# Row maxima of grouped heads: one product of 128 rows per head, or two of 64 rows side by side

## The chip, the cores and the metric

The kernel runs on one core of one Trainium2 chip. The metric is the device time of one execution, in microseconds (us); lower is better. A core has five engines with queues of their own: TensorE (PE; its weight loads are listed as PEld), VectorE (DVE), ScalarE (ACT), GpSimd (POOL) and SyncE (SP), which here starts the DMAs. TensorE writes its products to PSUM, eight banks of 128 partitions x 512 numbers.

## The reference

Two layers of an encoder trunk on 512 tokens of width 1024, in float32. Each layer has three branches on the normed input (latent attention, grouped-query attention, pooling), each projected, gated and added, an output projection, and a gated feed-forward part with a depthwise convolution. The change concerns the grouped-query branch: 8 query heads of 64, 2 key heads, so four query heads share a key head.

```python
def gqa_branch(q_raw, k_raw, v_raw, qn_g, kn_g, cos, sin):
    q = q_raw.reshape(b, s, GQA_HEADS, GQA_HEAD_DIM)
    k = k_raw.reshape(b, s, GQA_KV_HEADS, GQA_HEAD_DIM)
    q = apply_rope(rms_norm(q, qn_g), cos, sin)
    k = apply_rope(rms_norm(k, kn_g), cos, sin)
    o = block_attention(q, k, v)
...
def one_block(qi):
    sc = jnp.einsum('bqgrd,bkgd->bgrqk', qi, k) * scale
    p = jax.nn.softmax(sc, axis=-1)
    return jnp.einsum('bgrqk,bkgv->bqgrv', p, v)
```

The softmax needs a number to subtract from each row of scores before the exponential. It cancels in the quotient, so it has only to be near the row's maximum.

## The kernel before, in words

**Precision.** Numbers are split into a high half (rounded to the format that TensorE multiplies in one pass) and a low half (the rest). A full product is three: high by high, high by low, low by high (`mm3`, L347). Weights stream from HBM through SP's queue into `raw`; ScalarE makes their high halves `wh`, GpSimd or VectorE the low halves `wl`.

**The order is written by a planner.** The program has no loop on the chip: Python writes every instruction, and each engine runs its own in that order. While it writes, a model (`Clock`) keeps estimated times of the engines and of events. `chain` places the steps that follow a product (evacuations, copies, subtractions) into the queues when the model's time comes; `need(key)` moves the model's time to the moment when an event is estimated to be over; `ps(tag)` does the same for a free PSUM bank. PSUM has five tags: acc (2 banks), ST (2), AV (2), S (1) and mi (1). None of these estimates is seen by the chip: it only sees the order and its own semaphores.

**Attention.** `attention(kind, fill, ...)` runs once for grouped heads ("gqa") and once for latent heads ("mla") in each layer. Its steps are sorted by a position. One unit of position is one block of 128 keys, and head h has its scores at 4h to 4h+3:

- `t_q` (for grouped heads `t_pair`): four transposes bring the queries of two heads into mi. Then, head by head: `hi` copies 64 partitions out of mi into `qa`; `lo` subtracts, mi less the copy, into the other 64 partitions of `qa`, and copies the high half to `qb`. After the second head's subtraction mi is free. The order is hi, hi, lo, lo.
- `s_max`(h, b): scores of 128 queries by all 512 keys into bank S, and a `tensor_reduce` on VectorE that writes the negated row maximum into column b of `nm`.
- `m_row`(h): a product with the identity turns `nm` into rows (bank mi), which VectorE writes into four rows of `qb`.
- `probs`(h, k): scores with keys on the partitions, in ST, with the maxima subtracted by those rows; exponential, high half `ph`, low half `pl`.
- `av_hi`, `av_lo`: products with the values into AV; `o_out` after the last: copies, four reciprocals, a product, a split.

For grouped heads `qa` has high and low half of a head's queries on its 128 rows, and `ka` has the keys' high half twice, on rows 0 to 63 and 64 to 127. The even head of a pair has its high half on rows 0 to 63, the odd one on rows 64 to 127.

Between the steps stands **filler**: products of gates and branches that don't depend on this attention, in steps of mostly three products of 512 columns. Ahead of each attention step filler is made up to a target that grows with the position (positions below 0 count by PRO = 0.47). For grouped heads it has 104 steps in all, of which 16 (PRE_A) are made before. Then, as long as the step would have to wait by the planner's estimate, further filler steps are made, up to 35 (SLACK) ahead of the target. What a step waits for is told by `waits`: a list of events and one bank.

```python
PLAN = {"gqa": (0.006, 0.786, 0.986, 0.65, 3.252, 2.411, 4.57, 32.003),
...
            tq, tk, s0, ds, mr, ah, al, end = PLAN[kind]
```

With p0 = 4(h - 1), `t_q` stands at p0 + 0.006, the maxima at p0 + 0.986 + 0.65k, `m_row` at p0 + 3.252, `av_hi` at 4h + k + 2.411 and `av_lo` at 4h + k + 4.57.

## Time and profile before

| | |
|---|---|
| three runs | 1660.67, 1662.70, 1664.17 us |
| their median | 1662.7 us |
| profiled execution: its own time | 1662.54 us |
| profiled execution: span of the trace | 1660.7 us |
| products on TensorE | 7394 |
| reductions for maxima on VectorE | 128 of 684 ns (mean) |
| products for maxima of grouped heads | 64, in `ps_S<-ka,qa` |
| bytes moved by DMA | 145.40 MB |

How to read it: a row of the timeline gives start, duration, engine, line, operation, what it writes and reads, tile, shape, and how many neighbouring instructions were merged; behind it, in brackets, stands how long the engine sat idle before and what ended that. Line numbers are often those of helpers: L340 is `mm`, L344 the transposes, L208 ScalarE, L215 a `tensor_tensor`, L223 a reduction. Products are told apart by their tiles. Of a product the record's end is modelled, so records overlap; the distance of starts is what one costs. In the windows the last three columns are the granted clock of TensorE as a share, the DMA share and GB/s.

### The profile page before, as it was taken

The page shows a single profiled execution, that of the slowest core. Times are in us where ns is not written, and L with a number is a line of the kernel's source. Part 1 is how long each engine was busy: PE and PEld are TensorE (multiplying, and loading weights), DVE is VectorE, ACT ScalarE, POOL GpSimd, SP SyncE. Part 2 cuts the span into 40 slices and gives each one's busy share as a digit, 9 for nine tenths or more (in the row PEclk, how much of TensorE's full clock was granted, in tenths as well). Part 3 has the DMA queues.
Part 4 walks back from the last instruction along what each step waited for, and adds up shares of the span by engine and source line. Part 5 has one row for each costly group of instructions (what it writes and reads, how often), then busy time and mean ns, then how long its engine had stood idle before and what let it go on. Part 6 is the DMA issues. An engine that isn't in the chain of part 4 may idle for free.

```text
span 1660.7 us, 20300 instructions
## 1 busy us (share of the span) xinstructions
PE 1648.2 (99%) x7394; PEld 1339.3 (81%) x7394; DVE 918.7 (55%) x1428; ACT 773.2 (47%) x1366; POOL 921.5 (55%) x787
## 2 busy tenths in 40 slices
PE   9999999999999999999999999999999999999999
PEld 9887787778888888888888877877788888888887
DVE  6677866753356667621046678667542666666100
ACT  6357755553444444433244567555434444444221
POOL 4752754444666566654567537533546666666543
PEclk9999999999999999999999999999999999999999
DMA  5231121124333333233333211211232222323331
GB/s 179 89 96 36 58 74 51 38 64 134 108 89 93 98 92 99 89 114 108 103 103 99 73 37 56 73 52 38 83 126 99 99 90 90 101 90 99 110 115 57
DMA packets 44596, 145.40 MB, mean 88 GB/s; under 512 B 5073, under 2 KB 6353, under 8 KB 44497
## 3 DMA queue, kind: packets, MB, share of 16 engines
q1 hardware_dynamic: 44352, 144.10, 27.4%
q8 instruction: 58, 0.95, 0.2%
q14 instruction: 42, 0.34, 0.1%
q10 hardware_dynamic: 144, 0.01, 0.0%
HBM read 139.90 MB, written 4.19 MB: 87 GB/s over the span
## 4 chain that ended last, share of the span: by engine, by line
PE 96%; DVE 2%; ACT 1%; POOL 1%; issue 0%; POOLq 0%; DVEq 0%
PE ps_acc L340 42%; PE ps_ST L340 24%; PE ps_AV L340 24%; PE ps_S L340 3%; PE ps_mi L340 2%; PE ps_mi L344 1%; PE ps_mi L1395 0%; POOL wl L215 0%; POOL MQ L215 0%; DVE nm L223 0%; DVE rp L215 0%; DVE kb L215 0%; ACT ps_ST L208 0%; DVE pl L215 0%; ACT ph L208 0%
## 5 line engine op out<-in xcount | busy, mean ns | idle before, releaser
L215 POOL TENSOR_TENSOR wl<-raw,wh 128x512 fp32r<-128x512 f32 (+3 forms) x508 | 665.5, 1319 | 601.4 <-ACT wh L208 511.4
L208 ACT ACTIVATE wh<-raw 128x512 fp32r<-128x512 f32 (+3 forms) x522 | 314.9, 609 | 190.1 <-PE ps_ST L340 82.9
L219 DVE SCALAR_TENSOR_TENSOR a<-u,prm,a 128x512 f32<-128x512 f32 x176 | 240.8, 1369 | 79.4 <-ACT a L208 72.8
L340 PE MATMUL ps_acc<-HH,wh 128*128 128x512 f32 x592 | 234.5, 396 | 0.8 <-DVE XM L219 0.8
L340 PE MATMUL ps_acc<-HL,wh 128*128 128x512 f32 x592 | 234.5, 396 | 0.0
L340 PE MATMUL ps_acc<-HH,wl 128*128 128x512 f32 x592 | 233.9, 395 | 0.5 <-POOL wl L215 0.5
L340 PEld LDWEIGHTS ps_acc<-HH,wh 128*128 128x128 f32 x592 | 111.4, 188 | 28.1 <-issue 1.2
L340 PEld LDWEIGHTS ps_acc<-HH,wl 128*128 128x128 f32 x592 | 111.3, 188 | 27.5 <-POOL wl L215 1.0
L208 ACT ACTIVATE ps_ST<-ps_ST 128x512 f32<-128x512 f32 x128 | 74.6, 583 | 126.2 <-PE ps_ST L340 125.3
L340 PEld LDWEIGHTS ps_acc<-HL,wh 128*128 128x128 f32 x592 | 111.4, 188 | 25.6
L340 PE MATMUL ps_AV<-HL,wh 128*128 128x512 f32 x288 | 114.2, 396 | 0.0
L340 PE MATMUL ps_AV<-HH,wl 128*128 128x512 f32 x288 | 114.1, 396 | 0.0
L340 PE MATMUL ps_AV<-HH,wh 128*128 128x512 f32 x288 | 113.5, 394 | 0.0
L223 DVE TENSOR_REDUCE nm<-ps_S 128x1 fp32r<-128x512 f32 x128 | 87.5, 684 | 33.1 <-PE ps_S L340 32.1
L215 POOL TENSOR_TENSOR al<-a,ah 128x512 fp32r<-128x512 f32 x44 | 58.1, 1322 | 84.7 <-ACT ah L208 60.5
L215 DVE TENSOR_TENSOR pl<-ps_ST,ph 128x512 fp32r<-128x512 f32 x128 | 86.7, 679 | 30.4 <-ACT ph L208 29.4
L340 PE MATMUL ps_ST<-HL,wh 128*128 128x512 f32 x240 | 95.2, 396 | 0.0
L340 PE MATMUL ps_ST<-HH,wl 128*128 128x512 f32 x240 | 94.9, 396 | 0.0
L340 PE MATMUL ps_ST<-HH,wh 128*128 128x512 f32 x240 | 94.6, 394 | 0.0
L208 ACT ACTIVATE a<-u,prm 128x512 f32<-128x512 f32 x88 | 71.8, 816 | 31.0 <-DVE u L215 30.9
L208 ACT ACTIVATE ah<-a 128x512 fp32r<-128x512 f32 x44 | 27.8, 631 | 117.0 <-DVE u L239 111.6
L208 ACT ACTIVATE a<-a 128x512 f32<-128x512 f32 x44 | 27.8, 633 | 114.2 <-DVE u L239 114.2
(344 smaller groups left out, 3565.3 us busy)
## 6 DMA issues: line engine op xcount, KB each, us to landing
raw<-w SPq DMA_DIRECT2D x228, 512.0 KB, 3.5
raw<-w SPq DMA_DIRECT2D x13, 384.0 KB, 3.1
XM<-x SPq DMA_DIRECT2D x16, 256.0 KB, 3.8
raw<-w SPq DMA_DIRECT2D x6, 448.0 KB, 3.4
xsp<-XM SPq DMA_DIRECT2D x8, 256.0 KB, 2.0
XM<-xsp SPq DMA_DIRECT2D x8, 256.0 KB, 3.4
out<-XM SPq DMA_DIRECT2D x8, 256.0 KB, 2.0
raw<-w SPq DMA_DIRECT2D x4, 432.0 KB, 3.2
```

The source lines that it names most:

```text
L208: return self.eng.activation(out, in_, func, **k)
L215: return self.eng.tensor_tensor(out, *a)
L219: return self.eng.scalar_tensor_tensor(out, *a)
L223: return self.eng.tensor_reduce(out, in_, *a, **k)
L340: PE.matmul(o, lhsT=lhsT, rhs=rhs, start=start, stop=stop)
L344: PE.transpose(o, src, ident)
```

## The change

Grouped heads get `s_pair` in place of `s_max`. It makes the maxima of heads h and h+1 (h even) for one block of queries: two products of 64 rows each, with the high half of the queries alone. The even head uses rows 0 to 63 of TensorE and writes to mi, the odd one rows 64 to 127 and writes to S. Two reductions on VectorE follow, mi first. The products with the low half of the queries are left out of these maxima.

Each `hi` now announces its own event, `qh`, and `s_pair` needs the two `qh`. `waits` names these two events and the bank S for it. The planner's model counts 0.232 us for a pair (a product of 512 columns counts 512/2370 = 0.216 us).

`nm` gets four buffers in place of two, in the latent heads too. For grouped heads `t_q` moves two units ahead, to p0 - 1.994, and `s_pair` stands at p0 - 1.014 + 1.2k. Latent heads keep `s_max` and their positions.

```diff
-                    def hi(qa=qa, own=own):
+                    def hi(i=i, qa=qa, own=own):
                         copy(qa[own, :T], tp[own])
+                        done(*key("qh", h + i))
...
-                    s["nm"] = small("nm", [P, 4], F32R)
+                    s["nm"] = small("nm", [P, 4], F32R, bufs=4)
...
+            def s_pair(h, b):
+
+                for i, tag in enumerate(("mi", "S")):
+                    s = hs[h + i]
+                    need(key("qh", h + i))
+                    if b == 0:
+                        s["nm"] = small("nm", [P, 4], F32R, bufs=4)
+                two = [ps("mi"), ps("S")]
+                for i, sc in enumerate(two):
+                    s, o = hs[h + i], 64 * i
+                    PE.matmul(sc, lhsT=s["qa"][o:o + 64, b * P:b * P + P], rhs=s["ka"][o:o + 64, :T],
+                              start=True, stop=True, tile_position=(o, 0))
+                ck.to(ck.now + 0.232)
+
+                def red(i):
+                    V.tensor_reduce(hs[h + i]["nm"][:, b:b + 1], two[i], AX.X, ALU.max, negate=True)
+                    free(("mi", "S")[i])
+                    done(*key("nm", h + i, b))
+                chain(lambda: red(0), lambda: red(1))
...
-                plan += [(p0 + tq, t_q, (h,)), (p0 + tk, t_k, (h,)),
+                plan += [(p0 + tq - 2.0 * gqa, t_q, (h,)), (p0 + tk, t_k, (h,)),
                          (p0 + mr, m_row, (h,))]
                 for k in range(4):
-                    plan += [(p0 + s0 + ds * k, s_max, (h, k)), (p0 + 4 + k, probs, (h, k)),
+                    plan += [(p0 + 4 + k, probs, (h, k)),
                              (p0 + 4 + k + ah, av_hi, (h, k)), (p0 + 4 + k + al, av_lo, (h, k))]
+                    if not gqa:
+                        plan.append((p0 + s0 + ds * k, s_max, (h, k)))
+                    elif h % 2 == 0:
+                        plan.append((p0 + s0 - 2.0 + 1.2 * k, s_pair, (h, k)))
...
+                if fn is s_pair:
+                    return [key("qh", h), key("qh", h + 1)], "S"
```

## The prediction

> **What bounds the kernel now.** I read the page's engine rows and its chain of waits first.

> ```profile
> span 1660.7 us, 20300 instructions
> PE 1648.2 (99%) x7394; PEld 1339.3 (81%) x7394; DVE 918.7 (55%) x1428; ACT 773.2 (47%) x1366; POOL 921.5 (55%) x787
> ...
> PE 96%; DVE 2%; ACT 1%; POOL 1%; issue 0%; POOLq 0%; DVEq 0%
> PE ps_acc L340 42%; PE ps_ST L340 24%; PE ps_AV L340 24%; PE ps_S L340 3%; PE ps_mi L340 2%; PE ps_mi L344 1%; PE ps_mi L1395 0%; POOL wl L215 0%; POOL MQ L215 0%; DVE nm L223 0%; DVE rp L215 0%; DVE kb L215 0%; ACT ps_ST L208 0%; DVE pl L215 0%; ACT ph L208 0%
> ```

> TensorE makes 96% of the chain that ended last, and the maxima's bank ps_S has 3% of it. A product removed is time gained, and a wait of TensorE is time lost at its full length. The windows then separate the stages: the two grouped-head stages (106:222 and 927:1050) and the two latent stages behind them.

> ```profile
> 106.00:222.00 116.00, 114.25 (x525) 91.09 (x526) 88.33 (x140) 82.39 (x150) 60.14 (x72) 1.00 0.17 51
> 222.00:448.00 226.00, 226.00 (x1020) 181.51 (x1019) 123.41 (x185) 108.61 (x193) 105.11 (x93) 1.00 0.26 81
> ...
> 927.00:1050.00 123.00, 117.83 (x535) 93.48 (x535) 93.72 (x147) 82.30 (x150) 62.50 (x75) 0.99 0.17 52
> 1050.00:1180.00 130.00, 130.00 (x604) 103.88 (x603) 86.46 (x133) 69.42 (x126) 57.72 (x56) 1.00 0.17 56
> ```

> Columns are the stretch, its length, and busy time of PE, PEld, DVE, ACT, POOL. TensorE is never without work in the latent stages; in the grouped ones it misses 1.75 and 5.17 us. VectorE is 76% busy there (88.3 of 116.0, 93.7 of 123.0), the highest of any stage but not a bound. The waits of TensorE in the second grouped stage are mainly two:

> ```profile
> PE ps_acc L340 <- POOL wl L215: 2.5, 1, 2.5
> PE ps_mi L340 <- DVE nm L223: 1.9, 1, 1.9
> ```

> **Step 1: two products become a pair.** Each layer has 32 products for the maxima of grouped heads, 64 in all, each with 128 rows (high and low halves). The change issues as many, with 64 rows each, two at a time on different rows of TensorE. What one costs now, from the timeline:

> ```profile
> 110.04 0.39 PE L340 MATMUL ps_acc<-HH,wl 128*128 128x512 f32 x1
> 110.04 0.19 PEld L340 LDWEIGHTS ps_S<-ka,qa 128*128 128x128 f32 x1
> ...
> 110.27 0.40 PE L340 MATMUL ps_S<-ka,qa 128*128 128x512 f32 x1
> 110.27 0.19 PEld L340 LDWEIGHTS ps_acc<-wh,cth 128*128 128x128 f32 x1
> 110.50 0.34 PE L340 MATMUL ps_acc<-wh,cth 128*128 128x384 f32 x1
> ...
> 118.20 0.22 PE L340 MATMUL ps_mi<-idr,nm 128*4 128x128 f32 x1
> 118.20 0.19 PEld L340 LDWEIGHTS ps_acc<-oph,wh 128*128 128x128 f32 x1
> 118.26 0.44 PE L340 MATMUL ps_acc<-oph,wh 128*128 128x512 f32 x1
> ...
> 118.54 0.40 PE L340 MATMUL ps_acc<-opl,wh 128*128 128x512 f32 x1
> ```

> The records of 0.39 us overlap: starts are 0.23 us apart (110.04, 110.27, 110.50), so a pair costs 0.46 us now. A weight load starts when the product before it starts, and hides under it. Where that product is short (118.20, next start 0.06 us later) the one after takes 0.28 in place of 0.23 us, so a load lasts 0.06 + 0.05 = 0.11 us.

> The trace has no product on half the rows, so the pair is bounded. If both loads hide and both products run at once, a pair is one product, 0.23 us: 32 x 0.23 = 7.4 us gained. If the second load begins only when the first product does, the second product starts 0.11 us later: 0.34 us, 3.9 us gained. If the products don't overlap, 0.46 us and nothing. I take the middle of the two with overlap, 0.29 us: a gain of 32 x 0.174 = **5.6 us**.

> A change of the array's shape might cost as well. The nearest row is the second product of the weighted sums, which uses 64 of the columns between products that use 128:

> ```profile
> 986.39 0.62 PE L340 MATMUL ps_AV<-ph,vg 128*128 128x512 f32 x2
> ...
> 986.85 0.40 PE L340 MATMUL ps_AV<-pl,vg 128*128 128x512 f32 x1
> ```

> Two products, the second on 64 columns, take 0.46 us: nothing is added. The other bound is that each change empties the array, at most what a record lasts beyond the spacing (0.40 - 0.23 = 0.17 us), twice a pair: 32 x 0.33 = 10.5 us. I take nothing, by the nearer row, and keep the other end as a rival. [...]

> **Step 2: the bank of the first pair.** The pair needs mi and S; mi still holds the pair's transposed queries. Before, the first maxima waited for the rows' subtraction and copy (key q), and only S was asked for. Now they wait for the two copies of high halves alone (key qh), and the planner, which steps filler while a step waits, looks at S but not at mi. So TensorE's queue gets the pair after the copies, and must wait there until the second subtraction has read mi. Everything on TensorE is queued behind: the filler's weight products, scores, weighted sums. For heads 0 and 1 the place is the same as before:

> ```profile
> 106.67 0.60 PE L344 MATMUL ps_mi<-C,gqr 128*128 128x128 f32 x4
> ...
> 107.30 1.21 ACT L208 ACTIVATE qa<-ps_mi 64x512 fp32r<-64x512 f32 x2 [0.95 <-PE ps_mi L344]
> ...
> 108.54 1.41 DVE L215 TENSOR_TENSOR qa<-ps_mi,qa 64x512 fp32r<-64x512 f32 x2 [1.61 <-ACT qa L208]
> 108.69 0.34 PE L340 MATMUL ps_acc<-wh,ctl 128*128 128x384 f32 x1
> ...
> 108.87 0.39 PE L340 MATMUL ps_acc<-HH,wh 128*128 128x512 f32 x1
> ```

> The copies end at 108.51, the filler step then running ends at 108.87, and mi is free at 109.95: a wait of 1.1 us (a gap of 1.44 us less 0.36 us of filler). The later pairs show how long the gap gets when VectorE is loaded:

> ```profile
> 128.88 1.20 ACT L208 ACTIVATE qa<-ps_mi 64x512 fp32r<-64x512 f32 x2
> 131.89 0.69 DVE L215 TENSOR_TENSOR qa<-ps_mi,qa 64x512 fp32r<-64x512 f32 x1
> 152.99 0.60 ACT L208 ACTIVATE qa<-ps_mi 64x512 fp32r<-64x512 f32 x1
> 155.02 0.95 DVE L235 RECIPROCAL osum<-osum 128x128 f32<-128x128 f32 x1
> 156.76 0.69 DVE L215 TENSOR_TENSOR qa<-ps_mi,qa 64x512 fp32r<-64x512 f32 x1
> ```

> Heads 2 and 3: copies end 130.08, mi free 132.58, gap 2.5 us. Heads 4 and 5: 153.59 to 157.45, 3.9 us, with a reciprocal of an earlier output between the subtractions. That collision goes: the reciprocals follow av_lo of head 1 at position 4 + 3 + 4.57 = 11.57, and the transposes move from 12.006 to 10.006. So for the six later pairs (three a layer) I take the middle of 1.5 and 2.5 us, 2.0, less 0.4 us of filler: 1.6 us. Sum: 2 x 1.1 + 6 x 1.6 = **11.8 us** lost. Ends: nothing, if the filler running at that moment covers the gap; 2 x 1.1 + 6 x 3.5 = 23 us, if each meets the longest gap.

> **Step 3: the rest of the order.** The m_row of an even head stands 0.67 units behind its last maxima (3.252 against 2.586) where it stood 0.32 (2.936), and for odd heads more. The wait of 1.9 us of ps_mi for nm (quoted above) is of that kind; I take it as gone: -1.9 us (end: 0). In exchange the m_row of the earlier odd head (7.252) now falls between the first and second pair of the next heads (6.986, 8.186), both on mi:

> ```profile
> 118.46 0.68 DVE L215 TENSOR_TENSOR qb<-ps_mi,C 4x512 fp32r<-4x512 f32 x1 [1.09 <-PE ps_mi L340]
> ```

> Its row product at 118.20 holds mi until 119.14, 0.94 us, within 1.2 units of about 3 us (the first window's 116.0 us hold some 36 units); its own wait for mi is covered by filler. I put 1.0 us on misses (0 to 6 x 0.94). The 64 reductions stay 64, so VectorE has no more work; the copies and subtractions are the same; no DMA is added or removed, and no queue but TensorE's is passed in another way than by the earlier transposes, whose copies come 2 units earlier on ScalarE and VectorE, which have room (71% and 76%). Four buffers for nm cost space only.

> **Sum.** The profiled execution took 1662.54 us (span 1660.7), the median of the runs is 1662.7. 1662.5 - 5.6 + 11.8 - 1.9 + 1.0 = **1667.8 us**.

> **Rivals.**
> (a) mi is free in time, and the change is faster. Place: the eight first pairs; it decides where the filler, scores or weighted sums that TensorE still has when the pair is issued last as long as the gap, 1.5 us, two filler steps of 0.70 us. For it: between transposes and maxima 0.98 units of plan lie, and if the filler isn't ahead of its target the planner puts about 2.5 steps there (104 steps less the 16 made before, over 34.8 units, times 0.98). Against: after heads 0 and 1 the copies were over within two steps. Price: 11.8 us less, 1656.0 us.
> (b) The pair doesn't overlap (the change doesn't do what it says): 5.6 us more, 1673.4 us. For it: nothing in the trace shows two products at once. Against: nothing does either, as none has fewer than 68 rows.
> (c) Each change of rows empties the array: 10.5 us more, 1678.3 us. Against it stands the product on 64 columns.
> (d) Long waits slow the clock too:

> ```profile
> 991.72 0.28 PE L340 MATMUL ps_acc<-wh,cth 128*128 128x256 f32 x1
> ...
> 994.47 0.46 PE L340 MATMUL ps_acc<-wl,cth 128*128 128x256 f32 x1 [2.47 <-POOL wl L215]
> ...
> 995.60 0.63 PE L340 MATMUL ps_ST<-qa,ka 128*128 128x512 f32 x1
> ...
> 996.02 0.63 PE L340 MATMUL ps_ST<-qb,kb 68*128 68x512 f32 x1
> ```

> After 2.5 us without work products of 512 start 0.42 us apart (995.60, 996.02), not 0.23. Some eight products lose 0.19 us: 1.5 us on each wait of that length. With two such waits, of 2.5 in place of 1.6 us: 1667.8 + 2 x (0.9 + 1.5) = 1672.6 us.

> **How the numbers follow.** Forecast (waits of 1 to 2 us on mi, some overlap) 0.45, its own range 1663 to 1672; (a) 0.28; (b) 0.12; (c) 0.08; (d) 0.07. The range of 8 in 10 reaches from 1655.5, just under (a), to 1676, above (b) and (d), and leaves (c) out and the far side of (a). What counts as a difference is 0.2%, 3.3 us (1659.4 to 1666.0). (a) gives faster, 0.28; of the forecast's 0.45 the part under 1666.0, 0.20, is the same; its other 0.25 with (b), (c) and (d) is slower, 0.52.

> **What would show it.** Step 1: starts of the two maxima products 0.00 to 0.11 us apart and the next start 0.23 us behind; equal spacing of 0.23 would be (b), a hole before or after each pair (c). Step 2: rows of TensorE's waits that name ps_mi for qa's subtraction, some 1 to 2 us, eight times; none means (a). Step 3: no wait of ps_mi for nm over 0.5 us. The forecast is wrong above all if the planner happens to place enough filler between copies and pair, or if the new order removes other waits of the grouped stages, 6.9 us in all now.

## The result, and the profile after

| | before | after |
|---|---|---|
| median | 1662.99 us (4 runs) | 1671.41 us (4 runs, 1670.79 to 1673.45) |
| ratio, 95% interval | | 1.0053 (1.0041 to 1.0066) |
| profiled execution: its own time | 1662.54 us | 1673.45 us, the longest of the four |
| the two grouped-head stages | 255.01 us | 264.58 us |

The change makes the kernel slower by 8.4 us. The profiled execution's granted clock is 0.999, that of the other three 1.000: it alone holds the stretch of slow clock that is shown below. The page of the kernel after, its engine rows and the chain of waits that ended last:

```profile
span 1671.6 us, 20309 instructions
PE 1653.4 (99%) x7394; PEld 1331.6 (80%) x7394; DVE 914.9 (55%) x1431; ACT 768.7 (46%) x1360; POOL 923.5 (55%) x790
...
PE 95%; issue 2%; DVE 1%; ACT 1%; POOL 0%; POOLq 0%
```

As many products as before (7394), and TensorE still makes the chain. New in it are 2% of "issue": time in which the engine waits for nothing that the profile can name. Before it was 0%.

To find the place, each layer is cut at two events that both kernels have: the first transposes of grouped queries, and the first transposes of latent queries. Between them lies the grouped-head stage. The windows of the kernel before, then of the kernel after (columns: stretch, length, busy time and instructions of PE, PEld, DVE, ACT, POOL, granted clock, DMA share, GB/s):

```profile
106.66:231.51 124.85, 123.10 (x565) 98.27 (x564) 93.60 (x148) 85.63 (x156) 65.32 (x77) 1.00 0.18 54
927.28:1057.44 130.16, 124.99 (x565) 99.25 (x564) 97.32 (x151) 84.21 (x152) 66.97 (x80) 0.99 0.18 56
```

```profile
107.62:240.47 132.85, 126.67 (x565) 95.26 (x564) 93.64 (x151) 82.69 (x151) 66.67 (x79) 0.99 0.17 51
936.36:1068.09 131.73, 125.26 (x565) 94.40 (x564) 94.57 (x151) 82.72 (x151) 67.71 (x81) 1.00 0.18 56
```

The same 565 products take 132.85 + 131.73 = 264.58 us in place of 255.01: 9.57 us more. The stretch between the two windows is 695.8 us before (231.51 to 927.28) and 695.9 after, the stretch from the second to the end of the span 603.3 and 603.5. Ahead of the first window TensorE's order is the same in both, and this execution took 1.0 us longer there (107.62 against 106.66). So what the change does lies in these two windows.

**The pair.** From the timeline of the kernel after, a pair that waits for nothing, with its weight loads:

```profile
113.86 0.34 PE L340 MATMUL ps_acc<-wh,ctl 128*128 128x384 f32 x1
114.13 0.18 PEld L1129 LDWEIGHTS ps_mi<-ka,qa 64*128 64x128 f32 x1 [0.26 <-issue]
114.13 0.50 PE L1129 MATMUL ps_mi<-ka,qa 64*128 64x512 f32 x1
114.13 0.50 PE L1129 MATMUL ps_S<-ka,qa 64*128 64x512 f32 x1
114.56 0.51 PE L340 MATMUL ps_acc<-HH,wh 128*128 128x512 f32 x1
114.56 0.19 PEld L340 LDWEIGHTS ps_acc<-HH,wh 128*128 128x128 f32 x1 [0.25 <-issue]
114.67 0.19 PEld L340 LDWEIGHTS ps_acc<-HL,wh 128*128 128x128 f32 x1
114.90 0.40 PE L340 MATMUL ps_acc<-HL,wh 128*128 128x512 f32 x1
```

The two products do run at once: they start in the same hundredth of a microsecond (3 to 4 ns apart). What is lost lies around them. The product ahead, of 384 columns, is followed after 0.27 us where its kind is elsewhere followed after 0.18 (111.07 to 111.25 in the kernel of full rows, below). The pair is followed after 0.43 us, not 0.23, and the product behind it after 0.34. In the mean over the pairs these are +0.10, +0.20 and +0.11 us, some 0.40 us for a visit (once into the products of 64 rows and back out). The loads show what differs: the pair's own load starts with the pair at 114.13, and the load of the next weights at 114.56, with their product. Elsewhere a load starts a product early (114.67, ahead of 114.90). On the way into the products of 64 rows and out of them it does not. One pair thus takes 0.23 + 0.40 = 0.63 us; the two products that it replaces took 0.46. By rows like these, 32 x 0.17 = 5.4 us; summed over the start distances around all 32 pairs, 5.7 us.

**The bank.** TensorE's waits in the kernel after (idle time in total, times, longest):

```profile
PE ps_mi L1129 <- DVE qa L215: 8.7, 5, 2.5
PE ps_mi L1129 <- ACT mqs L208: 2.1, 2, 1.1
...
PE ps_mi L1129 <- ACT wh L208: 1.1, 1, 1.1
```

L1129 is the pair, and eight waits are the eight first pairs. Five name the subtraction of `qa`. The other three name operations of ScalarE (`mqs`, `wh`) that read and write nothing of the pair's; in the timeline of the kernel after, at heads 0 and 1:

```profile
109.50 1.39 DVE L215 TENSOR_TENSOR qa<-ps_mi,qa 64x512 fp32r<-64x512 f32 x2 [1.62 <-ACT qa L208]
...
110.53 0.48 ACT L208 ACTIVATE mqs<-ps_acc 128x384 f32<-128x384 f32 x1
...
111.04 0.47 PE L1129 MATMUL ps_mi<-ka,qa 64*128 64x512 f32 x1 [1.06 <-ACT mqs L208]
```

The subtractions end at 109.50 + 1.39 = 110.89, and the pair starts 0.15 us later. It starts 0.15 us behind the second subtraction at all eight places, so it is the same wait in the three. The operation named here ends at 111.01, by chance just ahead of the pair. One of the long ones, heads 2 and 3, and what follows it:

```profile
130.37 0.40 PE L340 MATMUL ps_acc<-HH,wl 128*128 128x512 f32 x1
...
131.29 0.69 DVE L215 TENSOR_TENSOR gt<-ps_acc,rbc 128x512 f32<-128x512 f32 x1
132.01 0.69 DVE L215 TENSOR_TENSOR qa<-ps_mi,qa 64x512 fp32r<-64x512 f32 x1
132.85 0.47 PE L1129 MATMUL ps_mi<-ka,qa 64*128 64x512 f32 x1 [2.08 <-DVE qa L215]
...
133.31 0.79 PE L340 MATMUL ps_ST<-qa,ka 128*128 128x512 f32 x1
133.90 0.63 PE L340 MATMUL ps_ST<-qb,kb 68*128 68x512 f32 x1
134.33 0.63 PE L340 MATMUL ps_acc<-oph,wh 128*128 128x512 f32 x1
134.75 0.63 PE L340 MATMUL ps_acc<-opl,wh 128*128 128x512 f32 x1
...
136.65 0.39 PE L340 MATMUL ps_acc<-oph,wh 128*128 128x512 f32 x1
136.88 0.39 PE L340 MATMUL ps_acc<-opl,wh 128*128 128x512 f32 x1
```

An operation of a gate (`gt`, 131.29) stands ahead of the second subtraction on VectorE, so mi is free at 132.01 + 0.69 = 132.70. Starts then are 0.42 to 0.43 us apart (133.90, 134.33, 134.75) until they are 0.23 again (136.65, 136.88): the clock is slow after the wait, 0.50 from 133.20 to 136.61 (the windows at the end of this document).

Measured by start distances, less the 0.10 us that any pair costs ahead, the eight waits take 12.4 us.

**The balance of the two windows**, by start distances: +5.7 for the pairs, +12.4 for the waits on mi. All other waits, slow clock included, fell from 13.7 to 5.2 us: -8.5. Those of 2.5 and 1.9 us that the prediction quotes are gone, and so is the slow clock behind the first. Together +9.6 us, which is the 9.57 of the windows. Both profiled executions hold one stretch of slow clock: before behind the wait of 2.5 us (0.50 from 994.64 to 998.05), after behind the wait at heads 2 and 3 (0.50 from 133.20 to 136.61).

### The profile page after: what moved, and what is told of

Its sections match the earlier page's. It is cut to its first block, busy times and chain, and to the rows that moved or that the text cites. A ratio compares the mean times of both kernels' runs of the same rounds, so it can differ in the third digit from the quotient of the medians.

```text
span 1671.6 us, 20309 instructions
## 1 busy us (share of the span) xinstructions
PE 1653.4 (99%) x7394; PEld 1331.6 (80%) x7394; DVE 914.9 (55%) x1431; ACT 768.7 (46%) x1360; POOL 923.5 (55%) x790
## 4 chain that ended last, share of the span: by engine, by line
PE 95%; issue 2%; DVE 1%; ACT 1%; POOL 0%; POOLq 0%
PE ps_acc L340 42%; PE ps_ST L340 24%; PE ps_AV L340 23%; PE ps_S L340 2%; PE ps_mi L340 2%; PE ps_mi L344 1%; PE ps_mi L1129 1%; PE ps_mi L1422 0%; POOL wl L215 0%; DVE qa L215 0%; ACT qa L208 0%; ACT qb L208 0%; ACT ps_ST L208 0%; DVE kb L215 0%; DVE ka L231 0%
## 5 line engine op out<-in xcount | busy, mean ns | idle before, releaser
L215 POOL TENSOR_TENSOR wl<-raw,wh 128x512 fp32r<-128x512 f32 (+3 forms) x511 | 668.9, 1317 | 613.8 <-ACT wh L208 543.9
L208 ACT ACTIVATE wh<-raw 128x512 fp32r<-128x512 f32 (+3 forms) x522 | 314.8, 609 | 190.7 <-PE ps_ST L340 84.2
L340 PE MATMUL ps_acc<-HH,wh 128*128 128x512 f32 x592 | 235.7, 398 | 0.8 <-DVE XM L219 0.7
L340 PE MATMUL ps_acc<-HL,wh 128*128 128x512 f32 x592 | 234.5, 396 | 0.0
L340 PE MATMUL ps_acc<-HH,wl 128*128 128x512 f32 x592 | 233.7, 395 | 0.3 <-POOL wl L215 0.3
L208 ACT ACTIVATE ps_ST<-ps_ST 128x512 f32<-128x512 f32 x128 | 74.1, 581 | 143.9 <-PE ps_ST L340 143.5
L340 PEld LDWEIGHTS ps_acc<-HH,wh 128*128 128x128 f32 x592 | 111.3, 188 | 30.6 <-issue 3.6
L340 PEld LDWEIGHTS ps_acc<-HH,wl 128*128 128x128 f32 x592 | 111.2, 188 | 27.4 <-POOL wl L215 0.7
L340 PEld LDWEIGHTS ps_acc<-HL,wh 128*128 128x128 f32 x592 | 111.4, 188 | 25.2
L340 PE MATMUL ps_AV<-HL,wh 128*128 128x512 f32 x288 | 114.1, 396 | 0.0
L340 PE MATMUL ps_AV<-HH,wl 128*128 128x512 f32 x288 | 114.0, 396 | 0.0
L340 PE MATMUL ps_AV<-HH,wh 128*128 128x512 f32 x288 | 113.4, 394 | 0.0
L215 DVE TENSOR_TENSOR pl<-ps_ST,ph 128x512 fp32r<-128x512 f32 x128 | 86.8, 680 | 38.6 <-ACT ph L208 34.8
L215 POOL TENSOR_TENSOR al<-a,ah 128x512 fp32r<-128x512 f32 x44 | 58.2, 1322 | 84.8 <-ACT ah L208 62.6
L340 PE MATMUL ps_ST<-HL,wh 128*128 128x512 f32 x240 | 95.1, 396 | 0.0
L340 PE MATMUL ps_ST<-HH,wl 128*128 128x512 f32 x240 | 94.9, 395 | 0.0
L340 PE MATMUL ps_ST<-HH,wh 128*128 128x512 f32 x240 | 94.6, 394 | 0.0
L208 ACT ACTIVATE a<-u,prm 128x512 f32<-128x512 f32 x88 | 71.8, 816 | 31.2 <-DVE u L215 31.1
L208 ACT ACTIVATE ah<-a 128x512 fp32r<-128x512 f32 x44 | 27.8, 631 | 116.9 <-DVE u L239 111.5
L208 ACT ACTIVATE a<-a 128x512 f32<-128x512 f32 x44 | 27.8, 632 | 114.1 <-DVE u L239 114.1
L223 DVE TENSOR_REDUCE nm<-ps_S 128x1 fp32r<-128x512 f32 x96 | 65.1, 678 | 14.8 <-PE ps_S L340 14.8
```

Of the source, the lines that this page charges most:

```text
L208: return self.eng.activation(out, in_, func, **k)
L215: return self.eng.tensor_tensor(out, *a)
L223: return self.eng.tensor_reduce(out, in_, *a, **k)
L340: PE.matmul(o, lhsT=lhsT, rhs=rhs, start=start, stop=stop)
```

## Experiments

Each time below is a median, set against the median of the kernel before, measured beside it on the same chip; "+" is slower. What the planner counts for a pair shifts its estimates, and with them the places of filler, so an edit there moves much that isn't meant. The clean readings are four couples whose instructions stand in the same order on every engine: the change and the change with each pair twice; before and before with single products of 64 rows; full rows and 64 rows in that order; the first experiment and full rows counted too low.

### Asking for both banks

Theory: the waits on mi come from the planner, which steps filler while S is taken but not while mi is. As in the kernel after, the maxima leave out the low halves of the queries.

```diff
-                    return [key("qh", h), key("qh", h + 1)], "S"
+                    return [key("qh", h), key("qh", h + 1)], ("mi", "S")
...
-                return not ck.has(*keys) or (tag and not (banks[tag] and banks[tag][0] <= ck.now))
+                tags = (tag,) if isinstance(tag, str) else tag or ()
+                return not ck.has(*keys) or any(not (banks[t] and banks[t][0] <= ck.now) for t in tags)
```

> The changed kernel, but the planner also asks whether bank mi is free before it issues a pair, and steps filler until then. Theory (the eight first pairs make TensorE wait for the subtractions that read mi, 1.2 to 2.6 us each, 12.4 us in the changed kernel's trace): these waits fall under 0.5 us each and the time falls by 8 to 12 us, to 1660 to 1664 us. Rival (the waits only move: the filler used up here is missing further on, or other waits of the grouped stages take their place): the eight waits go, other waits of TensorE grow by as much, and the time stays within 3 us of 1671.4.

1671.45 against 1663.16 us: +8.3, ratio 1.0053 (1.0038 to 1.0068), the same as the change. The waits on mi are gone, but nothing is gained, as the rival said. Its waits and its timeline:

```profile
PE ps_ST L340 <- DVE pl L215: 4.7, 4, 2.7
```

```profile
206.75 0.40 PE L340 MATMUL ps_acc<-oph,wl 128*128 128x512 f32 x1
...
214.97 0.80 PE L340 MATMUL ps_ST<-qa,ka 128*128 128x512 f32 x1 [2.71 <-DVE pl L215]
```

The product at 206.75 is the last of the filler; from there to 227.65 us only maxima, their rows, scores and weighted sums are left, and TensorE waits for VectorE's low halves of the probabilities (`pl`). The theory fails: the filler that covers mi is missing at the end of the stage.

### Each pair twice

What does a pair cost by itself, and what the change of rows around it? Each pair is issued twice into the same banks; the reductions stay.

```diff
-                for i, sc in enumerate(two):
+                for i, sc in list(enumerate(two)) * 2:
```

> The changed kernel with the two products of each pair issued twice, one after the other (even, odd, even, odd), nothing else touched; the planner counts the same, so the order is the same. Theory (the extra cost of a pair, about 0.40 us beyond the 0.235 us that it computes, is paid once for entering and once for leaving the mode of 64 rows): 32 x 0.235 = 7.5 us more than the changed kernel, about 1679 us. Rival (each pair pays it, because its two weight loads can't hide): 32 x 0.63 = 20 us more, about 1691 us.

1681.32 us, +18.2, ratio 1.0108 (1.0091 to 1.0125): 9.7 us more than the change's +8.4, nearer the price for each visit than for each pair. Its timeline:

```profile
113.13 0.50 PE L1129 MATMUL ps_mi<-ka,qa 64*128 64x512 f32 x1
...
113.47 0.39 PE L1129 MATMUL ps_mi<-ka,qa 64*128 64x512 f32 x1
...
113.79 0.50 PE L340 MATMUL ps_acc<-HH,wh 128*128 128x512 f32 x1
114.13 0.39 PE L340 MATMUL ps_acc<-HL,wh 128*128 128x512 f32 x1
```

The second pair starts 0.34 us behind the first; its loads start at 113.24, 0.11 us behind the first pair. It is left after 0.32 in place of 0.43 us. A second pair in one visit costs 0.334 + 0.323 - 0.428 = 0.23 us, a first one 0.63. That makes 32 x 0.23 = 7.3 of the 9.7 us. The other 2.4 us are mostly slow clock: the granted clock of its profiled execution (1681.53 us) is 0.998, where the change's, with one slow stretch, has 0.999, and three of the four executions are at 0.998 or 0.999. The one at 1.000 took 1678.93 us, 7.5 us above the change's median, which is at 1.000 too.

### Full rows, two heads at a time

The opposite split: the change's positions, its use of mi as a second bank and its four buffers of `nm`, with products of all 128 rows. They need the subtraction, so they wait for `q`, as before; mi is free by then. The maxima take in the low halves again.

```diff
-                    need(key("qh", h + i))
+                    need(key("q", h + i))
...
-                    s, o = hs[h + i], 64 * i
-                    PE.matmul(sc, lhsT=s["qa"][o:o + 64, b * P:b * P + P], rhs=s["ka"][o:o + 64, :T],
-                              start=True, stop=True, tile_position=(o, 0))
-                ck.to(ck.now + 0.232)
+                    s = hs[h + i]
+                    mm(sc, s["qa"][:, b * P:b * P + P], s["ka"][:, :T], True, True)
...
-                    return [key("qh", h), key("qh", h + 1)], "S"
+                    return [key("q", h), key("q", h + 1)], "S"
```

> The changed kernel's positions and banks (two heads at a time, mi and S, two units ahead), but with products of 128 rows, high and low halves, as before the change; so the pair waits for the low halves too, by which time mi is free. Theory (the mode of 64 rows costs 0.17 us a pair net, the wait for mi 12.4 us, and the earlier positions themselves take waits out of the grouped stages): 1671.4 - 5.5 - 12 = about 1654 us, under the kernel before by some 8 us. Rival (the earlier positions bring nothing of their own): 1660 to 1665 us, as before the change.

1660.20 against 1663.16 us (10 and 13 runs): -3.0, ratio 0.9983 (0.9973 to 0.9992). The theory's figure is not reached; the rival's range is, at its low end. It is the fastest kernel of this study, by 0.17%, and the interval leaves 1 out. About half of this gain is the slow clock behind the wait of 2.5 us, which costs the kernel before some 1.6 us by start distances: the ten executions of full rows all have a granted clock of 1.000, twelve of the 13 of the kernel before 0.998 or 0.999, and its one execution at 1.000 took 1660.54 us.

### Full rows against 64 rows in one order

The kernel above, with nothing changed but the products, and no change in what the planner counts for them. The maxima leave out the low halves, though they are there.

```diff
-                    s = hs[h + i]
-                    mm(sc, s["qa"][:, b * P:b * P + P], s["ka"][:, :T], True, True)
+                    s, o = hs[h + i], 64 * i
+                    PE.matmul(sc, lhsT=s["qa"][o:o + 64, b * P:b * P + P], rhs=s["ka"][o:o + 64, :T],
+                              start=True, stop=True, tile_position=(o, 0))
+                    ck.to(ck.now + T / 2370.0)
```

> e3_full_rows with nothing but its products changed: 64 rows each, the low halves of the queries left out, side by side as in the changed kernel; order, waits and counts are the same. Theory (a visit to the mode of 64 rows costs 0.40 us more than its 0.235 us of work, so a pair 0.17 us more than two products of 128 rows): 32 x 0.17 = 5.4 us more than e3_full_rows, about 1665.6 us. Rival (the pairs' net cost in the changed kernel was an effect of its waits, and side by side they gain as planned): 4 to 7 us less than e3_full_rows, 1653 to 1656 us.

1664.39 against 1663.38 us: +1.0, ratio 1.0007 (0.9997 to 1.0016). Against the kernel of full rows that is 1.0 + 3.0 = 4.0 us more. No pair waits for mi in either, every engine has the same order in both, and all executions of both are at a clock of 1.000: this is the price of the products of 64 rows. First pair of full rows, then of 64 rows, each from its kernel's timeline:

```profile
111.07 0.34 PE L340 MATMUL ps_acc<-wh,ctl 128*128 128x384 f32 x1
111.25 0.40 PE L340 MATMUL ps_mi<-ka,qa 128*128 128x512 f32 x1
111.48 0.40 PE L340 MATMUL ps_S<-ka,qa 128*128 128x512 f32 x1
111.72 0.40 PE L340 MATMUL ps_acc<-HH,wh 128*128 128x512 f32 x1
111.95 0.40 PE L340 MATMUL ps_acc<-HL,wh 128*128 128x512 f32 x1
```

```profile
110.82 0.34 PE L340 MATMUL ps_acc<-wh,ctl 128*128 128x384 f32 x1
111.09 0.50 PE L1129 MATMUL ps_mi<-ka,qa 64*128 64x512 f32 x1
111.09 0.50 PE L1129 MATMUL ps_S<-ka,qa 64*128 64x512 f32 x1
111.52 0.50 PE L340 MATMUL ps_acc<-HH,wh 128*128 128x512 f32 x1
111.86 0.39 PE L340 MATMUL ps_acc<-HL,wh 128*128 128x512 f32 x1
```

From the product ahead to the second product behind: 0.88 us with two full products, 1.04 us with the pair. 32 x 0.16 = 5.1 us by these rows; 4.0 us come through to the end.

### Single products of 64 rows

The kernel before, with its maxima made by one product of 64 rows at a time, in identical order; the low halves are left out of the maxima.

```diff
-                mm(sc, s["qa"][0:kd, b * P:b * P + P], s["ka"][0:kd, :T], True, True)
+                if gqa:
+                    o = 64 * (h % 2)
+                    PE.matmul(sc, lhsT=s["qa"][o:o + 64, b * P:b * P + P], rhs=s["ka"][o:o + 64, :T],
+                              start=True, stop=True, tile_position=(o, 0))
+                    ck.to(ck.now + T / 2370.0)
+                else:
+                    mm(sc, s["qa"][0:kd, b * P:b * P + P], s["ka"][0:kd, :T], True, True)
```

> The kernel before, in its order, but each of the 64 products for maxima of grouped heads has 64 rows (high halves alone, the low halves of the queries are left out of the maxima), one at a time in bank S. Theory (entering and leaving the mode of 64 rows costs about 0.40 us each visit, whatever is done in it): 64 x 0.40 = 25 us more than before, about 1688 us, with a start distance of 0.43 us behind each product and none of the loads begun ahead. Rival (the cost is that of a second weight load which finds no product to hide under): within 3 us of before, 1660 to 1666 us.

1682.86 against 1663.16 us: +19.7, ratio 1.0122 (1.0107 to 1.0137); a product of half the rows, alone, makes the kernel slower by 0.31 us each. The rival, under which it costs as much as one of 128 rows, is out. Its timeline:

```profile
113.33 0.39 PE L340 MATMUL ps_acc<-HH,wl 128*128 128x512 f32 x1
113.65 0.49 PE L1112 MATMUL ps_S<-ka,qa 64*128 64x512 f32 x1
114.07 0.50 PE L340 MATMUL ps_acc<-HH,wh 128*128 128x512 f32 x1
114.41 0.39 PE L340 MATMUL ps_acc<-HL,wh 128*128 128x512 f32 x1
```

The distances 0.32, 0.42 and 0.34 us exceed 0.23 by the same 0.09, 0.19 and 0.11 as around a pair. So the cost hangs on the visit, with no part for the pair's second product. In starts it is 64 x 0.394 = 25.2 us; other waits shrank from 13.7 to 8.0 us, as whatever they wait for is further along when TensorE is slower. 25.2 - 5.7 = 19.5.

### Asked, with the pair's true price

The planner counts 0.232 us for a pair that takes 0.63. Here it asks for both banks, as in the first experiment, and counts 0.60.

```diff
-                ck.to(ck.now + 0.232)
+                ck.to(ck.now + 0.60)
```

> e1_mi_asked, but the planner counts 0.60 us for a pair, near what it takes (0.63), in place of 0.232. In e1_mi_asked the eight waits on mi went, but the filler was used up 20 us before the end of each grouped stage, and the scores then waited for the subtractions of the probabilities. Theory (a planner that counts too little time for a pair sees waits that aren't there and spends filler on them): filler lasts to the end of the stage, and the time falls to 1664 to 1667 us. Rival (the wait for mi costs its filler whatever the count, and the stage is short of filler): bare scores at the end of the stages as in e1_mi_asked, and 1669 to 1673 us.

1664.56 against 1663.38 us: +1.2, ratio 1.0008 (0.9999 to 1.0017), in the theory's range. No pair waits on mi, and the filler lasts to the end of the stage (its last product starts at 220.06). With both repairs the change is level with the kernel before in the medians, though only the kernel before has a slow clock in most executions; nine of these ten are at 1.000.

### The true price alone

The change with 0.60 counted, and mi not asked for.

> The changed kernel with the planner's count for a pair raised from 0.232 to 0.60 us, and mi still not asked for; it differs from e5_asked_counted in that question alone. Theory (the eight waits on mi are time of TensorE that nothing gives back as long as filler lasts): they stay, 8 to 12 us in sum, and the time is 1671 to 1676 us. Rival (a wait on mi only saves filler, which then covers a later wait): the eight waits stay, other waits shrink by as much, and the time is within 2.5 us of e5_asked_counted, 1662 to 1667 us.

1670.22 against 1663.05 us: +7.2, ratio 1.0039 (1.0024 to 1.0054), just under the theory's range, and above the rival's. The eight waits stay:

```profile
PE ps_mi L1129 <- DVE qa L215: 7.7, 5, 2.1
PE ps_mi L1129 <- ACT mqs L208: 2.1, 2, 1.1
...
PE ps_mi L1129 <- ACT wh L208: 1.1, 1, 1.1
```

So it is the missing question that makes the waits, and not the low count. Their 10.9 us (7.7 + 2.1 + 1.1) bring 7.2 - 1.2 = 6.0 us at the end, since the two grouped stages of this kernel have some 5 us less of other waits, by start distances, than those of the one that asks.

### Full rows, counted too low

Full rows, as above, with 0.232 us counted once for the two products, which take 0.46 (the expectation speaks of 0.232 for each product; the kernel counted it for the pair).

```diff
-                    mm(sc, s["qa"][:, b * P:b * P + P], s["ka"][:, :T], True, True)
+                    PE.matmul(sc, lhsT=s["qa"][:, b * P:b * P + P], rhs=s["ka"][:, :T], start=True, stop=True)
+                ck.to(ck.now + 0.232)
```

> e3_full_rows, but the planner counts 0.232 us a product (0.464 us a pair) in place of 0.216; a control on how much a small change of the planner's count moves the time by itself. Theory (orders that differ this little give the same time): within 2 us of 1660.2. Rival (the stages' waits depend on the order at random, several us from one order to the next): outside 1658 to 1662.5 us, in either direction.

1667.81 against 1663.38 us: +4.4, ratio 1.0026 (1.0016 to 1.0036). With the low count alone the kernel of full rows loses 4.4 + 3.0 = 7.4 us, and it does so as the first experiment did:

```profile
PE ps_ST L340 <- DVE pl L215: 6.1, 4, 3.0
```

Its order is that of the first experiment on every engine, and the two differ by rows alone: 8.3 - 4.4 = 3.9 us, a second measure of the price beside the 4.0 above, and a rougher one (the first experiment's four executions lie between 1670.14 and 1672.69 us).

### Full rows, 0.232 us for each product

The count that the expectation above meant.

```diff
+                    PE.matmul(sc, lhsT=s["qa"][:, b * P:b * P + P], rhs=s["ka"][:, :T], start=True, stop=True)
+                    ck.to(ck.now + 0.232)
```

> e3_full_rows with each of its maxima products counted 0.232 us in place of 0.216, so 0.464 us a pair. (The kernel of e8_full_low_count counted 0.232 us a pair, not a product as its expectation says; its order is that of e1_mi_asked.) Theory (a count near the measured one gives an order that keeps filler to the end of the stage): 1658 to 1662.5 us, and no bare scores at the end. Rival (the time hangs on the order at random, by several us at each small change of a count): outside that.

1660.92 against 1663.05 us: -2.1, ratio 0.9984 (0.9974 to 0.9994). A count of 0.232 in place of 0.216 us for each product does no harm, though it places filler elsewhere; so the gain of full rows doesn't hang on one order.

### The early transposes alone

The kernel before, with nothing but the transposes two units ahead.

```diff
-                plan += [(p0 + tq, t_q, (h,)), (p0 + tk, t_k, (h,)),
+                plan += [(p0 + tq - 2.0 * gqa, t_q, (h,)), (p0 + tk, t_k, (h,)),
```

> The kernel before, with the transposes of grouped heads alone two units ahead; maxima one head at a time, 128 rows, in S, at their old positions. Theory (what e3_full_rows gains on the kernel before comes from the transposes, whose subtractions no longer meet the reciprocals on VectorE): 1659 to 1662 us. Rival (it comes from the maxima, which stand two units ahead of their row products and so take the waits for nm away): no gain, 1662 to 1665 us.

1662.09 against 1663.38 us: -1.3, ratio 0.9990 (0.9981 to 1.0000). This lies at the border of both ranges and decides nothing: the transposes may bring part of the 3.0 us of full rows, or none.

## Why the prediction came out as it did

In steps from the kernel before to the kernel after, with the differences of each against its own kernel before:

| step | kernel reached | us |
|---|---|---|
| positions, second bank, four `nm` | full rows | -3.0 |
| products of 64 rows | 64 rows in that order | +4.0 |
| `qh`, both banks asked, true count | asked, true price | +0.2 |
| mi not asked | true price alone | +6.0 |
| 0.232 us counted | the change | +1.2 |
| sum | | +8.4 |

The steps don't add up in any order: the low count costs 1.2 us here, but 8.3 - 1.2 = 7.1 us where mi is asked for. And the first step holds the slow clock that the kernel before has and the others here mostly don't; against its one execution at a clock of 1.000 (1660.54 us) the three of the change at 1.000 are 10 to 11 us slower.

The forecast was 1667.8 us, +5.3 over its base; +8.4 was measured, in the range and of the sign that had the highest chance. Two of its terms were off by 11.3 and 7.6 us, in opposite directions; that the time still fell into the forecast's own range is in part luck.

**Step 1 failed.** "A change of the array's shape might cost as well ... I take nothing, by the nearer row". The row was a product on 64 columns, which added nothing to the 0.46 us of two products. It doesn't stand for a product on 64 rows: the trace has 0.40 us around each visit, and the step's gain of 5.6 us is a loss of 5.7 by start distances, 4.0 us at the end by both comparisons in one order. The difference to the forecast's term, 11.3 us, is close to the 10.5 us of rival (c), which had "each change of rows empties the array", and the hole before and after each pair is where "what would show it" put it for (c). So (c) had the place and nearly the size, at a chance of 0.08; that the array empties was the author's reading, which no run shows. The bound that the prediction called "at most", 0.33 us a visit, is passed by the 0.40 measured. Its time, 1678.3 us, wasn't reached mainly because other waits fell by more than it assumed. What the traces show is that no load starts ahead across the change of rows (114.13 and 114.56 above), and that a first pair takes 0.63 us where a second one in the same visit adds 0.23 (each pair twice).

**The overlap** itself was taken rightly, with the second product 0 to 0.11 us behind the first; it is 0.00. Rival (b) is out.

**Step 2 held.** Eight waits, on mi, at the first pairs, for the second subtraction: 12.4 us by start distances where 11.8 were forecast, 1.1 to 2.5 us each against "some 1 to 2". That the planner looks at S alone is shown by the pair of kernels that differ in this question: the waits stand with the true count, and vanish where mi is asked for. What the prediction didn't see ("a wait of TensorE is time lost at its full length") is that the lost time isn't all loss: what stands behind a wait finds its own waits shorter, so 10.9 us of waits are worth 6.0 at the end.

**Step 3 was half right.** The wait of 1.9 us for `nm` is gone, as said. The 1.0 us for `m_row` between two pairs didn't come: none of TensorE's waits after names it. And the largest gain had no term of its own: the wait of 2.5 us for a low half of weights went too, with the slow clock behind it; the prediction names the 6.9 us of other waits only among what could make it wrong. For the other waits -8.5 us stand where -0.9 (1.9 gone, 1.0 new) was forecast. Part of this is what full rows show without the change's faults (-3.0 us, about half of it slow clock); how much of the rest is chance of the order, and how much follows from mi as a second bank, stays open.

**Rival (a)**, mi free in time, was priced at 11.8 us less than the forecast. The kernel that makes it so, with the true count, is 1.2 us slower than before: without the waits there is nothing to gain, since the pair itself costs.

**Rival (d)** had the price right and the number of times too high: the slow clock is seen once, behind the wait at heads 2 and 3. From 133.31 to 136.65 the starts take 3.34 us where 1.80 would do at full speed, so 1.5 us are lost, as the rival had it. Behind the longest wait it isn't seen, and not at all in the three executions at a clock of 1.000.

## What to carry to other kernels

Work out products of half the rows by the visit and not by the product: between products of all rows, two products of half the rows side by side take 0.63 us here, and two of all rows 0.46; at 0.23 us for each further pair, a visit would have to hold at least two pairs to gain (an estimate: 0.86 us against 0.92 for four products of all rows; no run here gains by it). Where a step takes a second bank, whatever decides when to issue it must look at both. And a planner's count for a new instruction has to be measured first: 0.23 us too little on 32 pairs of full rows moved the filler and cost 7.4 us, nearly as much as the whole change.

## What the runs showed of the hardware

**64 rows and 64 columns differ.** A product on 64 of the columns between products on 128 costs nothing extra (in the prediction's rows the two, from 986.39 to 986.85, take 0.46 us, twice 0.23), one on 64 of the rows costs 0.39 us extra even alone (0.32, 0.42 and 0.34 us in place of three times 0.23). Not every smaller number of rows does: the 64 products on 68 rows in the kernel before start 0.23 us behind the product ahead, and are followed after 0.23 us (medians). Where each pair is issued twice, the second came 0.34 us behind the first (113.13 to 113.47).

**How long an idle time slows the clock** isn't a matter of its length alone. After 2.24 us (the time from the end of the last spacing, 130.61, to 132.85) the granted clock falls; after 2.64 us, measured in the same way (1012.38 to 1015.02), it doesn't. Four windows of the kernel after around the two, with the granted clock third from the end:

```profile
129.79:133.20 3.41, 1.33 (x7) 0.67 (x5) 2.79 (x5) 2.82 (x5) 0.00 (x0) 1.00 0.01 2
133.20:136.61 3.41, 3.41 (x10) 2.38 (x9) 1.95 (x3) 1.18 (x2) 1.27 (x1) 0.50 0.28 72
...
1010.43:1013.84 3.41, 2.12 (x13) 1.46 (x10) 2.90 (x5) 3.39 (x8) 3.41 (x4) 1.00 0.26 103
1013.84:1017.25 3.41, 2.23 (x10) 1.58 (x11) 3.23 (x6) 1.33 (x3) 3.33 (x5) 1.00 0.50 154
```

**The named releaser can be one that the product doesn't need.** Three of the eight waits are put down to ScalarE's `mqs` and `wh`. These end 0.03 us ahead of the pair, and so later than the subtraction, but the pair uses neither; all eight pairs start 0.15 us behind the end of their second subtraction.
